# Moving sixteen modulation products from the query stage into the gate stage, and finishing the latent tiles first in the output projection

## The chip, the cores and the metric

The kernel runs on one core of one Trainium2 chip. The metric is the device time of one execution in microseconds; the profile shows one such execution, instruction by instruction, with the time that each engine sat idle and what ended the idling.

## What is computed

Two layers (`DEPTH = 2`) over 256 latent tokens and 256 context tokens of width 1024. Cut to what matters:

```python
for l in range(DEPTH):
    m_lat = split(silu(c) @ ada_w[l] + ada_b[l], 6)        # six modulation rows of 1024
    m_ctx = split(silu(c_ctx) @ ada_w[l] + ada_b[l], 6)
    h  = rmsnorm(x, norm_mix[l]) * (1 + m_lat[1]) + m_lat[0]          # and the same for ctx
    f, p, q, k, v, gates = split_proj(h @ w_in[l])                    # three branches, three gates of 1024
    x  = x + m_lat[2] * ((g0 * yf + g1 * yp + g2 * ya) @ w_out[l])    # ctx too, in layer 0
    h2 = rmsnorm(x, norm_ffn[l]) * (1 + m_lat[4]) + m_lat[3]
    x  = x + m_lat[5] * peer(h2, peer_wq[l], peer_keys[l], peer_u[l], peer_v[l])
```

`peer` makes 8 queries of 256 for each token, scores them against 128 + 128 keys, takes the top 16 of the sums, and mixes the chosen experts of 16,384.

The modulation vector has 6 x 1024 columns. The kernel makes it in three groups of 2048 columns (group 0: `m[0]`, `m[1]`; group 1: `m[2]`, `m[3]`; group 2: `m[4]`, `m[5]`), each as eight products of 128 rows of `ada_w`. One product, `(l, g, k)` below, needs a 1 MB slab of `ada_w`. There are 48 in all.

## The kernel before

All fp32 products on TensorE are made from split operands: `split_to` writes a rounded part `hi` (ScalarE) and the rest `lo` (VectorE, or GpSimd where `pool` is set), and `mm3` (lines 282 to 284) runs three matmuls: hi by hi, one of the mixed products, and the other.

**Weights.** Every weight comes through the class `Stream`. Its list `items` fixes the order of all loads; each item is loaded into one of three buffers of 8 KB a partition (`raw`), issued by SyncE. `take(key)` hands out the next item and issues loads up to two items beyond it; a load waits until the buffer of the item three places earlier has been read. An item that is marked for it is split into a `hl` buffer; `split(key)` hands out a split item and at once splits the next one if that one is marked (`presplit`). Modulation slabs are not split: TensorE reads them from `raw`.

**A modulation product** is `ada_item`: four matmuls of 512 columns, in four column strips of the array, which the profile lists as eight records of line 333 (tile `adaps`). With `k == 0` it also loads the bias (four small loads, line 329). After `k == 7`, `finish` adds the bias on VectorE (line 340, tile `adab`) and SyncE writes the result to DRAM in four pieces (line 346, tile `md`), or `mix_cols` turns it (group 0). After `(0, 2, 7)`, `ffn_rows(0)` follows: SyncE reads rows of `md` back (line 398). Ahead of `(1, 0, 0)` stands `mix_gain(1)`: a small load of `norm_mix` (line 383) and a TensorE transpose of it (line 385).

**Stages of layer 0**, in the order in which they run on TensorE:

- group 0 of layer 0's modulation, the token projections, attention;
- the gate stage: 12 units of `rest`, each 48 matmuls of 512 columns. Ahead of unit `n` stand the modulation products of `ada_at[n]`, two for each unit: the 16 of layer 0's groups 1 and 2, and the 8 of layer 1's group 0;
- the output projection `wout(n, b)`: column block `n` of 4, token tile `b` of 4 (tiles 0 and 1 are latent, 2 and 3 context), then `wout_end(b)`, which stores the tile and computes its norm (`Norm.row`). `Norm.trans(s, q)` and `Norm.cols(s, q)` transpose, modulate and split the normed tiles of side `s` (0 latent, 1 context);
- the query stage: for each head `h` of 8, the query product of `wq` (48 matmuls of 512 columns; in head 0 they are run in two halves, with `nrm.cols(1, ...)` between them), the scores of the head before (tile `SC`), and a share of the top-16 selection on VectorE, handed out by `pump`. In this stage stand the 16 modulation products of layer 1's groups 1 and 2, ahead of the heads: 3, 2, 2, 3, 2, 2, 2;
- the expert stage: 64 steps of `u`, each with a transpose on VectorE (`u_T`, line 1009), splits on ScalarE and GpSimd (`u_hi`, `u_lo`), 48 matmuls and a share of the selection, then 64 steps of `v`.

Instructions of one engine run in the order in which the program writes them (`manual_schedule`). Those lines that the rest turns on:

```python
ada_at[n * len(rest) // 24].append(((0, 1 + n // 8) if n < 16 else (1, 0)) + (n % 8,))   # 242
...
raw_p = sp("raw", 3)
...
self.ahead(self.n + 3)                 # in Stream.take
...
for la, g, k in ada_at[n]:             # gate stage, ahead of each unit
    if (la, g, k) == (1, 0, 0):
        mix_gain(1)
    ada_now(la, g, k)
```

Of the kernel before, what the change touches and what calls it, by code (L numbers as in the profile page):

```python
# [60 lines left out]
def kernel(ctx_: ExitStack, tc: tile.TileContext, I, C, out):  # L61
    nc = tc.nc
    ctx = ctx_
    DEPTH = I["ada_w"].shape[0]
# [45 lines left out]
    def dram(ap_src, off, dims):  # L110
        return bass.AP(tensor=ap_src.tensor, offset=ap_src.offset + off, ap=dims)
# [62 lines left out]
    S = Stream()  # L174
# [5 lines left out]
    def unit_loader(name, l, rows, cols, c0, w=256):  # L180

        def fn(t):
            a = I[name]
            load(out=t[:, :rows // 128 * w].rearrange("p (k n) -> p k n", n=w),
                 in_=dram(a, l * rows * cols + c0, [[cols, 128], [128 * cols, rows // 128], [1, w]]))
        return fn
# [9 lines left out]
    def ada_loader(l, g, k):  # L196
        def fn(t):
            load(out=t, in_=dram(I["ada_w"], (l * D + k * 128) * 6 * D + g * 2048, [[6 * D, 128], [1, 2048]]))
        return fn
# [29 lines left out]
    def const_loader(name, w):  # L229
        def fn(t):  # L230
            load(out=t[:, :w], in_=C[name])
        return fn
# [6 lines left out]
    fills = [("gate", 0, 0), ("gate", 0, 1), ("gate", 0, 2), ("gate", 1, 0)]  # L239
    rest = [("proj", 0, 0)] + [u for u in units[4:] if u not in fills]  # L240
    ada_at = {n: [] for n in range(len(rest))}
    for n in range(24):
        ada_at[n * len(rest) // 24].append(((0, 1 + n // 8) if n < 16 else (1, 0)) + (n % 8,))

    def add_unit(l, u):
        kind, cp, i = u
# [5 lines left out]
    for l in range(DEPTH):  # L252
        if l == 0:
            for k in range(KD):
                S.add(("ada", 0, 0, k), ada_loader(0, 0, k), False)
        for u in (4, 2, 3, 0, 1):
            S.add(("tok", l, u), unit_loader("w_in", l, D, IN_COLS, u * 256), True)
        S.add(("mixc", l), const_loader("mixc", 1280), False)
        S.add(("band", l), const_loader("band", 2048), False)
        for u in fills:  # L260
            add_unit(l, u)
        for n, u in enumerate(rest):
            add_unit(l, u)
            if l == 0:
                for la, g, k in ada_at[n]:
                    S.add(("ada", la, g, k), ada_loader(la, g, k), False)
        for n in range(4):
            S.add(("wout", l, n), unit_loader("w_out", l, D, D, n * 256), True)
        S.add(("keys", l), keys_loader(l), False)
        for h in range(8):  # L270
            S.add(("wq", l, h), wq_loader(l, h), True)
            if l + 1 < DEPTH:
                for n in [n for n in range(16) if n * 7 // 16 == h]:
                    S.add(("ada", l + 1, 1 + n // 8, n % 8), ada_loader(l + 1, 1 + n // 8, n % 8), False)
        for st in range(NSTEP):
            S.add(("u", l, st), u_loader(l, st), False)
        for st in VORDER:
            S.add(("v", l, st), v_loader(l, st), True)
# [73 lines left out]
    def ada_now(l, g, k):  # L352
        f = ada_item(l, g, k)
        if f:
            f()
# [412 lines left out]
    def peer(l, nrm, kT, nb, fin):  # L768
# [261 lines left out]
        for h in range(9):  # L1030
            cur = None
            if h < 8:
                if l + 1 < DEPTH:
                    for n in [n for n in range(16) if n * 7 // 16 == h]:
                        ada_now(l + 1, 1 + n // 8, n % 8)
                wh, wl = S.split(("wq", l, h))
                wh = wh.rearrange("p (k n) -> p k n", n=256)
                wl = wl.rearrange("p (k n) -> p k n", n=256)
                q = b4([128, 2, na], name="q")
                pss = [psum(), psum()]  # L1040
                for c in ([slice(0, 256), slice(256, 512)] if h == 0 and nb == 4 else [slice(0, na)]):
                    if c.start:
                        for q4 in range(4):
                            nrm.cols(1, q4)
                    for p in range(2):
                        w = slice(p * 128, (p + 1) * 128)
                        for k in range(KD):
                            mm3(pss[p][:, c], wh[:, k, w], wl[:, k, w], h2h[:, k, c], h2l[:, k, c], k == 0, k == KD - 1)
                for p in range(2):
                    nc.scalar.activation(q[:, p, :], pss[p][:, :na], AF.Copy)  # L1050
                cur = q
            if prevq is not None:
                g = h - 1
                if g % 4 == 0:
                    SCT[g // 4] = b16([128, 4, 2, nb, 128], name="SC")
                sct = SCT[g // 4][:, g % 4]
                for p in range(2):
                    ps = psum()
                    for b in range(nb):
                        nc.tensor.matmul(ps[:, b * 128:(b + 1) * 128], lhsT=prevq[:, p, b * 128:(b + 1) * 128],  # L1060
                                         rhs=kT[:, 2 * g + p, :], start=True, stop=True)
                    nc.scalar.activation(sct[:, p], ps[:, :na].rearrange("p (b n) -> p b n", b=nb), AF.Copy)
                SC[g] = sct
                if g == 3 and sparse is not None:
                    token_rows()
                if g == 5:
                    u_T(0)
                if g == 6:
                    u_hi(0)
                    u_lo(0)  # L1070
                if g == 7:
                    for q in range(1, LEAD):
                        u_T(q)
                        u_hi(q)
                        u_lo(q)
                    u_T(LEAD)
                pump((15.0 if g < 5 else 9.0) if nb == 4 else (5.6 if g < 6 else 3.0))
            prevq = cur
# [111 lines left out]
    nrm = Norm(0, X, 4, False)  # L1190
# [11 lines left out]
    for l in range(DEPTH):  # L1202
        last = l == DEPTH - 1
        nb = 2 if last else 4
# [3 lines left out]
        def keys():  # L1208
            kT = b8([128, 16, 128], name="keysT")
            for q in range(4):  # L1210
                ps = psum()
                for a in range(4):
                    nc.tensor.transpose(ps[:, a * 128:(a + 1) * 128], kr[:, 4 * q + a, :], ident)
                nc.scalar.activation(kT[:, 4 * q:4 * q + 4, :], ps.rearrange("p (a n) -> p a n", a=4), AF.Copy)
            return kT
# [9 lines left out]
        nrm = Norm(l, X, nb, True)  # L1225
        xm = [dr_p.tile([128, D], F32, name=f"xm{l}_{b}") for b in range(nb)]

        def wout(n, b):
            wh = wo[n][0].rearrange("p (k n) -> p k n", n=256)
            wl = wo[n][1].rearrange("p (k n) -> p k n", n=256)  # L1230
            c = slice(n * 256, (n + 1) * 256)
            ps = psum()
            t = slice(b * 128, (b + 1) * 128)
            for k in range(KD):
                m = mg[k // 4][:, :, k % 4, t]
                mm3(ps[:, :256], m[:, 0], m[:, 1], wh[:, k, :], wl[:, k, :], k == 0, k == KD - 1)
            tm = b1([128, 256], name="tm")
            nc.vector.tensor_tensor(out=tm, in0=ps[:, :256], in1=m2[b // 2][:, c], op=OP.mult)
            nc.vector.tensor_tensor(out=X[:, b, c], in0=X[:, b, c], in1=tm, op=OP.add)

        def wout_end(b):
            nc.sync.dma_start(out=xm[b], in_=X[:, b, :])
            nrm.row(b // 2, b % 2)
# [5 lines left out]
                wout(n, b)  # L1249
        if nb == 4:  # L1250
            wo[2] = S.split(("wout", l, 2))
            for b in range(nb):
                wout(2, b)
            wo[3] = S.split(("wout", l, 3))
            kr = S.take(("keys", l)).rearrange("p (a d) -> p a d", d=128)
            for b in range(2):
                wout(3, b)
            wout_end(0)
            wout(3, 2)
            wout_end(1)  # L1260
            S.presplit(True)
            wout(3, 3)
            kT = keys()
            for q in range(4):
                nrm.trans(0, q)
            for b in (2, 3):
                wout_end(b)
            for q in range(4):
                nrm.cols(0, q)
        else:  # L1270
            wo[2] = S.split(("wout", l, 2))
            wo[3] = S.split(("wout", l, 3))
            kr = S.take(("keys", l)).rearrange("p (a d) -> p a d", d=128)
            wout(2, 0)
            wout(3, 0)
            wout_end(0)
            S.presplit(True)
            wout(2, 1)
            wout(3, 1)
            wout_end(1)  # L1280
            kT = keys()
            for q in range(4):
                nrm.cols(0, q)
# [35 lines left out]
        if not last:  # L1319
            nrm = nxt["nrm"]  # L1320
# [29 lines left out]
```

## Time and profile before

| | |
|---|---|
| three runs | 3004.71, 3005.0, 3011.52 us; median 3005.0 |
| the profiled execution | 3004.79 us; its span in the trace 3002.7 us |
| mean granted TensorE clock | 0.958 of full speed |
| busy over the span | TensorE 92%, VectorE 70%, ScalarE 46%, GpSimd 43% |
| traffic | 235 GB/s mean over the span |

Times in the trace count from the start of the span. A busy share says only how much of a stretch an engine worked; what sets the time is read from the waits: an engine's row in brackets shows how long it sat idle just before the instruction, and which engine or transfer ended that. L12 is line 12 of the program. DMA-issuing instructions on SyncE's queue are marked SPq.

### The profile page before, as it was taken

The page shows a single profiled execution, that of the slowest core. Times are in us where ns is not written, and L with a number is a line of the kernel's source. Part 1 is how long each engine was busy: PE and PEld are TensorE (multiplying, and loading weights), DVE is VectorE, ACT ScalarE, POOL GpSimd, SP SyncE. Part 2 cuts the span into 40 slices and gives each one's busy share as a digit, 9 for nine tenths or more (in the row PEclk, how much of TensorE's full clock was granted, in tenths as well). Part 3 has the DMA queues.
Part 4 walks back from the last instruction along what each step waited for, and adds up shares of the span by engine and source line. Part 5 has one row for each costly group of instructions (what it writes and reads, how often), then busy time and mean ns, then how long its engine had stood idle before and what let it go on. Part 6 is the DMA issues. An engine that isn't in the chain of part 4 may idle for free. (4 is left out here: it accounts for less than half of the span.)

```text
span 3002.7 us, 42583 instructions
## 1 busy us (share of the span) xinstructions
PE 2753.9 (92%) x16484; PEld 2419.2 (81%) x16484; DVE 2114.1 (70%) x3252; ACT 1372.8 (46%) x2243; POOL 1287.1 (43%) x674
## 2 busy tenths in 40 slices
PE   6999998798887879999999998899887998899999
PEld 4767786688887779988888887779887988888887
DVE  3444355898787765558999997646797889466666
ACT  3443222233488874333333333444444777544443
POOL 0110002247666557766666664110577676610000
PEclk8999999899988989999999999999998999999999
DMA  6215655657987879999999996426788799987775
GB/s 228 89 39 201 243 175 167 173 135 192 238 240 231 256 242 290 283 291 392 368 384 373 365 385 249 143 84 198 148 182 187 197 237 229 224 288 294 285 291 202
DMA packets 365579, 706.98 MB, mean 235 GB/s; under 512 B 25425, under 2 KB 265457, under 8 KB 351297
## 3 DMA queue, kind: packets, MB, share of 16 engines
q1 hardware_dynamic: 271104, 491.38, 54.8%
q0 software_dynamic: 36864, 134.23, 12.5%
q10 hardware_dynamic: 57408, 78.65, 7.6%
q8 instruction: 129, 2.11, 0.3%
q14 instruction: 74, 0.60, 0.1%
HBM read 619.18 MB, written 85.00 MB: 235 GB/s over the span
## 5 line engine op out<-in xcount | busy, mean ns | idle before, releaser
L1173 PE MATMUL acc<-hl,A 128*128 128x512 f32 x3840 | 870.9, 389 | 0.0
L1173 PEld LDWEIGHTS acc<-hl,A 128*128 128x128 f32 x3840 | 720.6, 188 | 149.9 <-ACT A L287 0.2
L1023 POOL TENSOR_TENSOR hl<-UT,hl 128x1024 fp32r<-128x1024 f32 x256 | 656.9, 2591 | 357.1 <-ACT hl L1016 348.6
L289 POOL TENSOR_TENSOR hl<-raw,hl 128x1024 fp32r<-128x1024 f32 x112 | 277.9, 2491 | 694.0 <-ACT hl L287 573.2
L287 ACT ACTIVATE hl<-raw 128x1024 fp32r<-128x1024 f32 x388 | 387.8, 1048 | 220.1 <-PE acc L1173 84.5
L289 DVE TENSOR_TENSOR hl<-raw,hl 128x1024 fp32r<-128x1024 f32 x276 | 354.1, 1315 | 120.8 <-ACT hl L287 120.4
L282 PE MATMUL ps<-hTh,hl 128*128 128x384 f32 (+2 forms) x1168 | 416.2, 356 | 24.7 <-ACT stg L924 17.9
L284 PE MATMUL ps<-hTh,hl 128*128 128x384 f32 (+2 forms) x1168 | 410.7, 352 | 9.1 <-POOL hl L1023 8.7
L283 PE MATMUL ps<-hTl,hl 128*128 128x384 f32 (+2 forms) x1168 | 409.7, 351 | 3.5 <-POOL hTl L289 3.5
L1009 DVE STREAM_TRANSPOSE UT<-raw 128x2048 f32<-128x2048 f32 x128 | 294.4, 2301 | 142.4 <-DMA raw<-in_peer_u_dram 110.0
L1016 ACT ACTIVATE hl<-UT 128x1024 fp32r<-128x1024 f32 x256 | 256.3, 1049 | 223.8 <-DVE UT L1009 207.6
L282 PE MATMUL ps<-hT,hl 128*128 128x256 f32 x1152 | 336.9, 292 | 20.5 <-ACT Hg L1128 13.2
L284 PE MATMUL ps<-hT,hl 128*128 128x256 f32 x1152 | 334.6, 290 | 16.7 <-POOL hl L1023 16.7
L283 PE MATMUL ps<-hT,hl 128*128 128x256 f32 x1152 | 333.0, 289 | 1.1 <-POOL hT L289 1.1
L282 PEld LDWEIGHTS ps<-hTh,hl 128*128 128x128 f32 x1168 | 231.8, 198 | 40.6 <-ACT stg L924 21.3
L287 ACT ACTIVATE A<-af 128x768 fp32r<-128x768 f32 (+1 forms) x128 | 94.5, 738 | 344.3 <-PE acc L1173 182.8
L282 PEld LDWEIGHTS ps<-hT,hl 128*128 128x128 f32 x1152 | 228.7, 199 | 23.3 <-ACT Hg L1128 15.0
L284 PEld LDWEIGHTS ps<-hTh,hl 128*128 128x128 f32 x1168 | 230.7, 197 | 18.3 <-POOL hl L1023 13.5
L284 PEld LDWEIGHTS ps<-hT,hl 128*128 128x128 f32 x1152 | 228.3, 198 | 20.1 <-POOL hl L1023 20.1
L962 DVE SCALAR_TENSOR_TENSOR picked<-picked,hrow 128x1024 f32<-128x1024 f32 x128 | 152.8, 1209 | 126.1 <-DMA picked<-in_peer_u_dram,picks 125.7
L283 PEld LDWEIGHTS ps<-hTl,hl 128*128 128x128 f32 x1168 | 231.9, 199 | 8.0 <-POOL hTl L289 3.7
L283 PEld LDWEIGHTS ps<-hT,hl 128*128 128x128 f32 x1152 | 228.5, 198 | 1.6 <-POOL hT L289 1.6
(246 smaller groups left out, 4651.8 us busy)
## 6 DMA issues: line engine op xcount, KB each, us to landing
raw<-in_peer_u_dram SPq DMA_DIRECT2D x512, 256.0 KB
raw<-in_peer_v_dram SPq DMA_DIRECT2D x128, 1024.0 KB
raw<-in_ada_w_dram SPq DMA_DIRECT2D x48, 1024.0 KB
G<-stg ACTq DMA_DIRECT2D x20, 2048.0 KB
raw<-in_w_in_dram SPq DMA_DIRECT2D x34, 1024.0 KB
Gq<-G SPq DMA_DIRECT2D x16, 1536.0 KB
H<-Hg ACTq DMA_DIRECT2D x56, 384.0 KB
Hq<-H SPq DMA_DIRECT2D x14, 1536.0 KB
```

Of the source, the lines that this page charges most:

```text
L282: nc.tensor.matmul(ps, lhsT=lh, rhs=rh, start=first, stop=False)
L283: nc.tensor.matmul(ps, lhsT=lh, rhs=rl, start=False, stop=False)
L284: nc.tensor.matmul(ps, lhsT=ll, rhs=rh, start=False, stop=last)
L287: nc.scalar.activation(hi, src, AF.Copy)
L289: eng.tensor_tensor(out=lo, in0=src, in1=hi.bitcast(F32), op=OP.subtract)
L962: nc.vector.scalar_tensor_tensor(row, row, 1.0, SP["h"], op0=OP.mult, op1=OP.mult, accum_out=dots[:, k:k + 1])
L1009: nc.vector.transpose(t, r)
L1016: nc.scalar.activation(t[:, 0, a], v[:, a], AF.Copy)
L1023: nc.gpsimd.tensor_tensor(out=t[:, 1, a], in0=v[:, a], in1=t[:, 0, a].bitcast(F32), op=OP.subtract)
L1173: nc.tensor.matmul(acc[b][n], lhsT=a4[:, lhs, a, t], rhs=rhs[:, o:o + 512], start=f, stop=e)
```

## The change

It does two things. The 16 modulation products of layer 1's groups 1 and 2 leave the query stage and join the 24 that stand in layer 0's gate stage: 40 over 12 units, which comes to 4, 3, 3, 4, 3, 3, 4, 3, 3, 4, 3, 3. The list of loads changes alike. And in layer 0's output projection, column blocks 2 and 3 are no longer run one after the other over all four tiles: both latent tiles are taken through blocks 2 and 3 first and normed, the transposes of the keys and of the latent side and its `cols` are put among the last products of the context tiles.

```diff
-    for n in range(24):
-        ada_at[n * len(rest) // 24].append(((0, 1 + n // 8) if n < 16 else (1, 0)) + (n % 8,))
+    for n in range(40):
+        ada_at[n * len(rest) // 40].append(((0, 1 + n // 8) if n < 16 else (1, n // 8 - 2)) + (n % 8,))
@@ list of loads, query stage
-            if l + 1 < DEPTH:
-                for n in [n for n in range(16) if n * 7 // 16 == h]:
-                    S.add(("ada", l + 1, 1 + n // 8, n % 8), ada_loader(l + 1, 1 + n // 8, n % 8), False)
@@ query stage, ahead of head h
-                if l + 1 < DEPTH:
-                    for n in [n for n in range(16) if n * 7 // 16 == h]:
-                        ada_now(l + 1, 1 + n // 8, n % 8)
@@ output projection, four tiles
             wo[2] = S.split(("wout", l, 2))
-            for b in range(nb):
-                wout(2, b)
             wo[3] = S.split(("wout", l, 3))
             kr = S.take(("keys", l)).rearrange("p (a d) -> p a d", d=128)
             for b in range(2):
+                wout(2, b)
                 wout(3, b)
-            wout_end(0)
+                wout_end(b)
+            S.presplit(True)
+            wout(2, 2)
             wout(3, 2)
-            wout_end(1)
-            S.presplit(True)
-            wout(3, 3)
             kT = keys()
+            wout(2, 3)
             for q in range(4):
                 nrm.trans(0, q)
+            for q in range(4):
+                nrm.cols(0, q)
+            wout(3, 3)
             for b in (2, 3):
                 wout_end(b)
-            for q in range(4):
-                nrm.cols(0, q)
```

## Rows read from the trace of the kernel before

**Rows 1.** Busy us of each engine (instructions) in the gate stage; then granted clock, DMA, GB/s.

```profile
238.40:395.90 157.50, 156.63 (x775) 112.83 (x774) 59.58 (x80) 43.12 (x54) 0.52 (x1) 1.00 0.71 250
```

**Rows 2.** Timeline of VectorE, from the first selection to the expert stage: start, us, instruction, [idle before].

```profile
494.35 0.29 DVE L791 MAX8 T1v<-SC 128x8 f32<-128x128 f32 x1 [19.94 <-ACT SC L1062]
...
540.61 0.29 DVE L791 MAX8 T1v<-SC 128x8 f32<-128x128 f32 x1 [7.69 <-ACT SC L1062]
...
580.33 0.29 DVE L791 MAX8 T1v<-SC 128x8 f32<-128x128 f32 x1 [1.79 <-ACT SC L1062]
581.17 0.68 DVE L791 MAX8 T1v<-SC 128x8 f32<-128x128 f32 x3 [0.54 <-ACT SC L1062]
...
591.14 0.66 DVE L340 TENSOR_TENSOR adab<-adaps,adab 128x512 f32<-128x512 f32 x1
...
629.07 2.28 DVE L1009 STREAM_TRANSPOSE UT<-raw 128x2048 f32<-128x2048 f32 x1
```

**Rows 3.** Timeline of ScalarE and TensorE at the third expert step.

```profile
631.38 2.00 ACT L1016 ACTIVATE hl<-UT 128x1024 fp32r<-128x1024 f32 x2 [9.02 <-DVE UT L1009]
...
632.49 0.63 PE L282 MATMUL ps<-hTh,hl 128*128 128x384 f32 x1 [2.33 <-ACT hl L1016]
```

**Rows 4.** Waits of SyncE's queue in the query stage: us in total, times, longest.

```profile
SPq L346 <- DVE adab L340: 35.6, 2, 27.2
```

**Rows 5.** Timeline of TensorE in the query stage: a modulation product after its load.

```profile
539.52 1.94 PE L333 MATMUL adaps<-raw,cT 128*32 128x512 f32 x8 [14.58 <-DMA raw<-in_ada_w_dram]
```

**Rows 6.** Timeline of TensorE: two modulation products in a row, and three.

```profile
329.39 1.92 PE L333 MATMUL adaps<-raw,cT 128*32 128x512 f32 x16
...
509.27 2.78 PE L333 MATMUL adaps<-raw,cT 128*32 128x512 f32 x24
```

**Rows 7.** A gate-stage load: SyncE's issues, and the stretch (last column GB/s).

```profile
304.52 1.19 SPq L198 DMA_DIRECT2D raw<-in_ada_w_dram  x2
...
304.50:308.60 4.10, 4.10 (x23) 2.74 (x16) 2.36 (x2) 1.80 (x2) 0.00 (x0) 1.00 0.76 256
```

**Rows 8.** Timeline of SyncE and TensorE at the kernel's start, the first eight products.

```profile
2.39 0.29 SPq L383 DMA_DIRECT2D mrows<-in_norm_mix_dram  x1
...
3.93 0.27 PE L385 MATMUL ps<-ident,mrows 8*128 8x8 f32 x1
...
9.70 11.86 SPq L198 DMA_DIRECT2D raw<-in_ada_w_dram  x5
...
16.74 1.94 PE L333 MATMUL adaps<-raw,cT 128*32 128x512 f32 x8 [3.03 <-DMA raw<-in_ada_w_dram]
```

**Rows 9.** Timeline of SyncE's queue around product (0, 2, 7).

```profile
330.52 0.33 SPq L198 DMA_DIRECT2D raw<-in_ada_w_dram  x1
332.16 1.15 SPq L346 DMA_DIRECT2D md<-adab  x4
...
337.12 0.32 SPq L383 DMA_DIRECT2D mrows<-in_norm_mix_dram  x1
```

**Rows 10.** TensorE after a short wait, and the stretch behind it (third column from the end: granted clock).

```profile
612.00 0.62 PE L284 MATMUL ps<-hTh,hl 128*128 128x384 f32 x1 [1.81 <-POOL hl L1023]
...
612.00:616.00 4.00, 4.00 (x14) 4.00 (x15) 4.00 (x15) 1.72 (x2) 2.87 (x2) 0.57 0.12 35
```

**Rows 11.** Timeline of TensorE between the output projection and head 0's second half.

```profile
454.72 4.64 PE L333 MATMUL adaps<-raw,cT 128*32 128x512 f32 x24 [8.30 <-DVE hTf L472]
...
468.12 0.66 PE L451 MATMUL ps<-ident,xn 128*128 128x128 f32 x4 [1.51 <-ACT hTf L474]
...
472.68 0.58 PE L283 MATMUL ps<-hTl,hl 128*128 128x256 f32 x1 [3.51 <-POOL hTl L289]
```

**Rows 12.** Timeline of GpSimd and VectorE: splits that TensorE waits for.

```profile
466.29 4.66 POOL L289 TENSOR_TENSOR hl<-raw,hl 128x1024 fp32r<-128x1024 f32 x2 [10.08 <-ACT hl L287]
...
385.50 2.36 DVE L289 TENSOR_TENSOR hl<-raw,hl 128x1024 fp32r<-128x1024 f32 x2
...
398.61 0.69 DVE L289 TENSOR_TENSOR mg<-gt,mg 128x512 fp32r<-128x512 f32 x1 [0.70 <-ACT mg L287]
```

## The prediction

> **What bounds the kernel now.** I read the busy times by stretch first. In the gate stage TensorE works 156.6 of 157.5 us [rows 1]: what is added there lengthens the stage, unless it waits besides. Then I read the waits. In the query stage TensorE once stands still for 14.58 us for a slab of `ada_w` [rows 5]. The slab is late because SyncE's queue, which issues every load in order, stands at the write of `md`, and that waits for VectorE's bias sum `adab`, 27.2 us at the longest [rows 4]: the sum is queued behind the top-16 selection. So the place from which the products are taken really has a fault.
>
> What that fault is worth is a second question. From the first selection at 494.35 VectorE is busy almost without a break: it idles when scores are late (7.69, 1.79 and 0.54 us [rows 2]) and otherwise works through to the transposes of the experts' first slabs. At the third expert step TensorE waits 2.33 us for ScalarE, and ScalarE has waited 9.02 us for VectorE's transpose of 629.07 [rows 2, 3]. So the query stage ends, for what comes after, when VectorE is through with its list, not when TensorE is. A gain on TensorE there counts only as far as VectorE starts earlier or idles less.
>
> **Added to the gate stage: 16 products.** Two in a row take 1.92 us, three 2.78 [rows 6]: 0.86 us for each further one. 16 x 0.86 = **+13.8 us**, with nothing to hide it, TensorE being full there.
>
> **Added waits: the fourth product of a unit.** Three `raw` buffers let two items be under way beside the one in use. With two products to a unit the ring holds exactly both slabs and the next unit's weights. With three it holds the three slabs when their turn comes; the unit's weights, and two slabs of the next turn, are then fetched during the 11 us of the unit, and the last slab when the weights have been split. I take this as just fitting: the last slab's load begins some 10 us into a period of about 14 and needs about 5 (below); the first two slabs of the turn cover the rest. With four slabs it can't fit: the fourth may be loaded only when the first is used up. SyncE issues that load 1.13 us after the turn begins (330.52 against 329.39 [rows 6, 9]). A slab needs 4.1 us from issue to the last byte on an idle queue (256 GB/s x 4.1 us = 1.05 MB [rows 7]); I add 1.0 us until TensorE sees it, an estimate from the kernel's start, where an issue at 9.70 serves a product at 16.74, 7.0 us later with two slabs ahead of it [rows 8]. So it is there 6.2 us after the turn began, and TensorE is through with three slabs after 2.78: a wait of 3.4 us. Bounds: 2.4 without the extra microsecond, 5.4 with the 7.0 us of the start. Behind the waiting product stands the whole unit; nothing else can run on TensorE.
>
> A short wait costs more than itself. After one of 1.81 us the granted clock falls to its lower level, 1.2 GHz: in the four us behind it, it averages 0.57 [rows 10], so 1.7 us of full-speed work are lost. I count 1.7 behind each wait, 0 as the bound. Units 0, 3, 6 and 9 have four products: 4 x (3.4 + 1.7) = **+20.4 us** (9.6 to 28.4).
>
> The Trainium skill, DMA: Bandwidth & Descriptors, section Anatomy of one DMA, fits a transfer as 2.0 us plus its bytes over 436 GB/s, which makes 4.4 us for a slab. By it the four waits would be 2.7 us each and the sum 2.8 us lower; the row gives 4.1 before any completion, and my sum keeps 5.1.
>
> **Moved past SyncE's queue: `mix_gain(1)`.** Product (0, 2, 7) and product (1, 0, 0) stood in different units, with 48 matmuls between them. Now both are in unit 4's turn: numbers 14, 15 and 16. After number 15 SyncE waits for the bias sum, writes `md`, waits until that has landed, reads the rows back, and only then issues the `norm_mix` rows, whose transpose stands ahead of number 16 on TensorE. In the rows that load is issued at 337.12, 5.8 us after number 15 ended (329.39 + 1.92), 0.4 of it a slab load that will stand elsewhere [rows 6, 9]. The same load took 1.5 us from issue to its transpose at the kernel's start [rows 8]. TensorE waits 5.4 + 1.5 = 6.9 us, with the clock 8.6: **+8.6 us** (6.4 to 11). Slabs are late there too, but inside this wait.
>
> **The stage's end.** The weights of output block 0 are now loaded into the buffer of the last unit's first slab. Issued 1.1 us into the turn, landed at 6.2 (their shorter rows make it rather 6.7), they are split by VectorE up to about 10 us into it, 4 us before TensorE leaves the stage at 13.9. Before, that split began at 385.50 and ended 8 us ahead of 395.9 [rows 1, 12]. Behind it on VectorE stand the last unit's six gate products, four sums and two splits, some 0.69 us each with 0.70 us of ScalarE ahead of each split [rows 12]: 9.7 us. The last split of `mg`, which the first output product needs about 3 us in, came 3.4 us in before and comes 5.7 in now. A wait of 2.5, with the clock **+4.2 us** (0 to 5).
>
> **Removed between output projection and head 1.** Before, TensorE stands idle 8.30 us for the latent norm, then runs three products in 4.64 [rows 11]. Now the latent tiles' norm falls behind four output products and the keys, and the transposes stand ahead of the last product. I take the whole wait as hidden. In head 0 the context side remains: its tiles now end last, its norm chain ends about 1 us after the first half of the head, and its low parts stand on GpSimd behind the split of head 1's weights, 4.66 us [rows 12]. That leaves some 4.1 us of the 1.51 + 3.51 [rows 11]. With the two products ahead of head 1 (1.85, counting their overlap): 8.3 + 4.6 + 0.9 + 1.85 = **-15.6 us** for the first scores, counted from the end of the gate stage. Bounds: -19.7 if the context wait goes too, -8 if half the latent wait is back.
>
> **Removed on VectorE.** With the products gone no `md` write stands in SyncE's queue, so scores come in time: 13.1 us for a head on TensorE against some 18 of selection. The idle 7.69 + 1.79 + 0.54 and two sums of 0.66 fall out [rows 2]: 11.3 us. TensorE's own removed time, 14.58 us and ten products more, is cover here and gives nothing beyond: TensorE merely waits longer at the third step. **-11.3 us** (-12 to -5, if another wait takes a part). Later stages have the same order of work and shift as a whole. The bias sums and `md` writes in the gate stage cost nothing more: VectorE is busy 59.6 of 157.5 us there [rows 1].
>
> **Sum.** 13.8 + 20.4 + 8.6 + 4.2 - 15.6 - 11.3 = +20.1 us. The profiled execution took 3004.8 (span 3002.7, 2.1 around it), 0.2 from the median of 3005.0: **3025 us**.
>
> **Rivals.**
> *The ring keeps up.* All waits in the gate stage vanish: 13.8 - 15.6 - 11.3 = -13.1, 2992 us. It needs a slab within 1.65 us of its issue (2.78 - 1.13), against 4.1 for the bytes alone, and the `norm_mix` rows ahead of time. With waits of W us in all the change gives W - 13.1; it is faster by over 0.3% (9 us, about what a measurement of this kernel can tell from no change) only where W stays under 4.1 us; I forecast 33.2. For it speaks only that three slabs never made TensorE wait in the query stage's second such turn [rows 6]. Chance 0.07.
> *Short waits, no clock.* W = 4 x 2.4 + 6.4 = 16, nothing at the stage's end: +2.9, 3008 us. Against it: 1.81 us of waiting sufficed for the clock [rows 10]. Chance 0.15.
> *VectorE's gain doesn't arrive*, because the step after is bound by something that the trace shows only as hidden now: +11.3 on the forecast, 3036 us. Against it: the chain of rows 2 and 3. Chance 0.10.
>
> The forecast has 0.68, with its own range 3013 to 3036. The bounds together give 3003 to 3046. The range 3002 to 3043 leaves out the fastest rival and the far end of the third. Faster by over 0.3%: 0.07; within it 0.17, the second rival and a bit of the forecast's low end; slower 0.76.
>
> **What would show it.** In the changed trace: the gate stage some 47 us longer, with four waits of `adaps` for a slab of 2.4 to 5.4 us in units 0, 3, 6 and 9, one of about 7 us before the `mix_gain` transpose in unit 4, and the granted clock at its lower level behind each; 8.3 us of idle gone ahead of head 0; no idle on VectorE from the first scores to the third expert step, and a longer wait of TensorE there. The prediction is wrong if `raw` slabs arrive in the turn, if TensorE reaches unit 4's transpose after its rows, or if the third step doesn't follow VectorE.

## The result and the profile after

The change makes the kernel slower: 3031.5 us (median of 5 runs, 3030.3 to 3043.7) against 3004.7 (5 runs, 3000.8 to 3011.5), a ratio of 1.0091 with a 95% interval of 1.0074 to 1.0108, or +26.8 us. The profiled execution took 3030.3 us, its span is 3028.5. Behind the edits its line numbers are 3 to 6 lower than before.

I cut both traces at the same events: the first modulation product of the gate stage, the first matmul of the output projection, the first `MAX8` of the selection, VectorE's transpose for the third expert step (629.07 in [rows 2]), the first of the 64 `v` steps, the end. The steps of `u` and of `v` are those of the expert stage. The gate stage before (before, e2, e10, e11) and the stretch from the first selection to the third expert step (the changed kernel, e1, e3 to e6) repeat to 0.1 us between kernels that share their code. The changed gate stage, with its waits, doesn't: it takes 202.7 to 206.9 us in the four kernels that have it as it is (the changed kernel, e1, e7, e12).

| us | before | after | difference | forecast |
|---|---|---|---|---|
| gate stage | 157.54 | 205.38 | +47.8 | +42.8 |
| its end to the first selection | 98.38 | 84.11 | -14.3 | +4.2 - 15.6 = -11.4 |
| first selection to third expert step | 134.72 | 134.29 | -0.4 | -11.3 |
| rest of the `u` steps | 712.0 | 705.4 | -6.6 | 0 |
| `v` steps and layer 1 | 1661.6 | 1660.6 | -1.0 | 0 |

**Gate stage.** First the busy times by stretch: us of TensorE, its weight loads, VectorE, ScalarE, GpSimd (instructions), then granted clock, DMA share, GB/s. The first line answers to [rows 1]; the next four are stretches in and behind the waits of units 3, 4, 6 and 9.

```profile
238.69:444.07 205.38, 181.87 (x904) 121.77 (x903) 59.60 (x79) 44.19 (x54) 1.05 (x2) 0.93 0.75 267
290.00:298.00 8.00, 5.27 (x23) 2.45 (x16) 0.71 (x1) 1.80 (x2) 0.00 (x0) 0.57 0.98 332
310.00:322.00 12.00, 5.12 (x17) 2.85 (x18) 3.73 (x5) 2.32 (x3) 0.24 (x1) 0.57 0.66 207
352.00:360.00 8.00, 7.13 (x24) 5.54 (x21) 3.58 (x9) 2.11 (x2) 0.52 (x1) 0.57 1.01 394
400.00:408.00 8.00, 6.87 (x22) 4.20 (x23) 2.16 (x2) 2.00 (x2) 0.00 (x0) 0.57 1.02 380
```

TensorE was full before (156.63 of 157.50). Now it stands idle for 23.5 us of a longer stage, and in the four stretches the granted clock is 0.57 on average. The waits themselves are in TensorE's timeline (start, us, instruction, idle before it and what ended that):

```profile
238.69 2.78 PE L330 MATMUL adaps<-raw,cT 128*32 128x512 f32 x24
244.78 1.06 PE L330 MATMUL adaps<-raw,cT 128*32 128x512 f32 x8 [3.31 <-DMA raw<-in_ada_w_dram]
...
289.59 1.07 PE L330 MATMUL adaps<-raw,cT 128*32 128x512 f32 x8 [2.76 <-DMA raw<-in_ada_w_dram]
293.39 1.94 PE L330 MATMUL adaps<-raw,cT 128*32 128x512 f32 x8 [2.73 <-DMA raw<-in_ada_w_dram]
...
296.27 0.63 PE L281 MATMUL ps<-yh,hl 128*128 128x512 f32 x1
...
297.92 0.39 PE L279 MATMUL ps<-yh,hl 128*128 128x512 f32 x1
...
316.88 0.24 PE L382 MATMUL ps<-ident,mrows 8*128 8x8 f32 x1 [7.42 <-DMA mrows<-in_norm_mix_dram]
...
351.25 1.06 PE L330 MATMUL adaps<-raw,cT 128*32 128x512 f32 x8 [3.08 <-DMA raw<-in_ada_w_dram]
...
401.13 1.94 PE L330 MATMUL adaps<-raw,cT 128*32 128x512 f32 x8 [3.14 <-DMA raw<-in_ada_w_dram]
...
448.09 0.38 PE L279 MATMUL ps<-hl,mg 128*128 128x256 f32 x1 [1.25 <-ACT mg L284]
```

(A turn is the row of products ahead of a unit.) Each turn of four products waits for its last slab, unit 3's for the last two. The same matmul takes 0.63 us behind a wait and 0.39 when the clock is back. On SyncE's queue stand the issues that end three of these waits:

```profile
239.82 0.35 SPq L198 DMA_DIRECT2D raw<-in_ada_w_dram  x1
...
312.86 2.17 SPq L395 DMA_DIRECT2D mrows<-md  x4
...
315.41 0.30 SPq L380 DMA_DIRECT2D mrows<-in_norm_mix_dram  x1
...
396.33 0.33 SPq L198 DMA_DIRECT2D raw<-in_ada_w_dram  x1
```

The fourth slab is issued 1.13 us into the turn and used 4.96 us (unit 0) and 4.80 us (unit 9) after its issue; the `norm_mix` rows 1.47 us after theirs. Unit 3 is the exception: its third slab was used 7.05 us after its issue, and its fourth 7.71. In unit 2's turn an `md` write and a bias load stand on SyncE's queue, and the first two slabs of unit 3 were issued 6.0 and 6.4 us after that turn began, where unit 2's own had been issued 2.0 and 2.9 after the one before. That this is why they were late is read from the order of the issues; no run tested it.

**From the first selection on.** The same stretch by engine, columns as above, of the kernel before and after:

```profile
494.35:629.07 134.72, 117.35 (x646) 94.85 (x645) 123.91 (x636) 31.34 (x44) 34.09 (x15) 0.92 0.55 145
```

```profile
528.18:662.47 134.29, 108.73 (x563) 95.56 (x561) 133.69 (x635) 31.53 (x44) 33.57 (x14) 0.90 0.28 59
```

VectorE's idle time did go, from 10.8 to 0.6 us, but its busy time rose by 9.8 us, with the two bias sums gone from it. The groups of VectorE's instructions by line (busy us, mean ns of one, idle before) show which took it, before and after:

```profile
L812 DVE TENSOR_TENSOR cand<-T1v 128x256 f32<-128x256 f32 x24 | 13.8, 611 | 0.0
```

```profile
L809 DVE TENSOR_TENSOR cand<-T1v 128x256 f32<-128x256 f32 x24 | 25.2, 1088 | 0.0
```

The `cand` adds of the selection make pairwise sums of two top-16 lists; they took 11.4 us more. One pair of them on VectorE's timeline before, with nothing beside it on GpSimd:

```profile
574.13 0.40 DVE L812 TENSOR_TENSOR cand<-T1v 128x256 f32<-128x256 f32 x1
...
574.45 0.41 DVE L812 TENSOR_TENSOR cand<-T1v 128x256 f32<-128x256 f32 x1
```

And one after:

```profile
543.73 1.70 DVE L809 TENSOR_TENSOR cand<-T1v 128x256 f32<-128x256 f32 x1
...
545.36 2.62 DVE L809 TENSOR_TENSOR cand<-T1v 128x256 f32<-128x256 f32 x1
```

GpSimd's timeline at that time, the low parts of the next head's query weights:

```profile
542.75 2.40 POOL L286 TENSOR_TENSOR hl<-raw,hl 128x1024 fp32r<-128x1024 f32 x1 [7.92 <-ACT hl L284]
...
545.10 2.59 POOL L286 TENSOR_TENSOR hl<-raw,hl 128x1024 fp32r<-128x1024 f32 x1
```

GpSimd's two end at 545.15 and 547.69, the two adds 0.28 and 0.29 later. An add that should take 0.4 us lasts until the GpSimd instruction beside it is over, and the profile books all of it as busy. The Trainium skill, SBUF — State Buffer, section "SBUF: two separate sides", states a rule that fits this: VectorE and GpSimd share one pair of SBUF ports under an exclusive lock; of a VectorE operation with two SBUF inputs and a GpSimd instruction that reads SBUF, the one that starts first keeps the pair for its whole length, and the other waits. The traces agree, here at 2.62 us for 0.41. The other order stands in the trace of before: a pair of adds that began at 565.12, 0.15 us ahead of GpSimd's split, took its usual 0.73 us, and the split 2.83 instead of 2.4.

TensorE, meanwhile, waits for VectorE. Its timeline at the first expert step and at the third, which answers to [rows 3]:

```profile
627.47 0.69 PE L279 MATMUL ps<-hTh,hl 128*128 128x384 f32 x1 [14.02 <-ACT hl L1013]
...
665.90 0.45 PE L279 MATMUL ps<-hTh,hl 128*128 128x384 f32 x1 [4.06 <-ACT hl L1013]
```

### The profile page after: what moved, and what is told of

Same layout as the page of the kernel before. It is cut to its first block, busy times and chain, and to the rows that moved or that the text cites. A ratio compares the mean times of both kernels' runs of the same rounds, so it can differ in the third digit from the quotient of the medians.

```text
span 3028.5 us, 42571 instructions
## 1 busy us (share of the span) xinstructions
PE 2760.8 (91%) x16484; PEld 2424.9 (80%) x16484; DVE 2129.0 (70%) x3252; ACT 1374.8 (45%) x2243; POOL 1288.3 (43%) x674
## 5 line engine op out<-in xcount | busy, mean ns | idle before, releaser
L279 PE MATMUL ps<-hTh,hl 128*128 128x384 f32 (+2 forms) x1168 | 415.5, 356 | 47.3 <-ACT hl L1013 27.2
L279 PE MATMUL ps<-hT,hl 128*128 128x256 f32 x1152 | 337.6, 293 | 17.9 <-ACT Hg L1122 11.3
L281 PE MATMUL ps<-hT,hl 128*128 128x256 f32 x1152 | 335.3, 291 | 16.7 <-POOL hl L1020 16.7
L959 DVE SCALAR_TENSOR_TENSOR picked<-picked,hrow 128x1024 f32<-128x1024 f32 x128 | 152.6, 1208 | 121.4 <-DMA picked<-in_peer_u_dram,picks 121.4
```

Of the source, the lines that this page charges most:

```text
L279: nc.tensor.matmul(ps, lhsT=lh, rhs=rh, start=first, stop=False)
L281: nc.tensor.matmul(ps, lhsT=ll, rhs=rh, start=False, stop=last)
L959: nc.vector.scalar_tensor_tensor(row, row, 1.0, SP["h"], op0=OP.mult, op1=OP.mult, accum_out=dots[:, k:k + 1])
```

## The experiments

Four groups: the two parts alone, the waits of the gate stage, VectorE's adds, and combinations. The table gives for each profiled execution the stage times in the cuts above, the busy time of the 24 `cand` adds, and the measured ratio.

| kernel | gate stage | to first selection | to third expert step | `cand` adds | third expert step at | median us, runs | ratio, 95% interval |
|---|---|---|---|---|---|---|---|
| before | 157.5 | 98.4 | 134.7 | 13.8 | 629.1 | 3004.7, 5 | |
| after | 205.4 | 84.1 | 134.3 | 25.2 | 662.5 | 3031.5, 5 | 1.0091 (1.0074 to 1.0108) |
| e1 | 205.5 | 92.9 | 134.3 | 25.2 | 671.2 | 3051.4, 4 | 1.0144 (1.0125 to 1.0164) |
| e2 | 157.5 | 94.1 | 135.1 | 16.7 | 626.2 | 2995.2, 5 | 0.9966 (0.9949 to 0.9982) |
| e3 | 197.9 | 83.8 | 134.3 | 25.2 | 654.0 | 3026.6, 4 | 1.0060 (1.0042 to 1.0079) |
| e4 | 191.1 | 82.7 | 134.3 | 25.2 | 646.9 | 3021.2, 10 | 1.0050 (1.0033 to 1.0066) |
| e5 | 186.3 | 82.3 | 134.3 | 25.2 | 640.4 | 3006.8, 1 | |
| e6 | 187.2 | 83.2 | 134.3 | 25.2 | 644.3 | 3013.1, 10 | 1.0028 (1.0017 to 1.0039) |
| e7 | 202.7 | 83.7 | 124.0 | 14.8 | 650.5 | 3022.4, 5 | 1.0056 (1.0037 to 1.0076) |
| e8 | 183.9 | 82.9 | 123.9 | 14.8 | 630.0 | 3002.2, 12 | 0.9995 (0.9983 to 1.0008) |
| e9 | 178.5 | 84.1 | 121.4 | 12.2 | 623.0 | 2997.2, 9 | 0.9969 (0.9957 to 0.9981) |
| e10 | 157.6 | 93.0 | 132.2 | 23.1 | 622.4 | 2994.2, 10 | 0.9974 (0.9962 to 0.9985) |
| e11 | 157.6 | 98.3 | 123.4 | 14.3 | 619.3 | 2989.0, 6 | 0.9953 (0.9941 to 0.9965) |
| e12 | 206.9 | 83.3 | 134.6 | 14.2 | 664.3 | 3036.6, 1 | |

The runs of the kernel before that stood beside e1 to e4 have a median of 3005.9, those beside e5 to e8 3004.9, those beside e9 to e12 3003.5; the ratios are taken to these. The rest of the `u` steps takes 702 to 716 us, and the `v` steps with layer 1 1658 to 1667, whatever the kernel, so a total holds 14 us and more that no stage of the change decides; the stage times are the finer instrument, save that a gain of under some 4 us on the changed gate stage can't be told from its own spread (above).

### e1: the products alone

The products stand in the gate stage, the output projection keeps its old order.

> Only the sixteen products are moved; the output projection runs in the old order. Theory (ring waits in the gate stage, and VectorE's gain in the query stage eaten by adds that wait for GpSimd): the gate stage is about 48 us longer than before, the 8.3 us idle ahead of head 0 is back, and from the first scores to the third expert step it takes as long as in the changed kernel, about 134 us; some 8 to 10 us above the changed kernel, 3038 to 3042 us. Rival (the new order of the output projection is what takes VectorE's gain): that stretch falls to about 124 us, and the time is at or under the changed kernel, 3026 to 3031 us.

The gate stage and the stretch behind the first selection are those of the changed kernel. The new order is worth 92.9 - 84.1 = 8.8 us of its -14.3; the products that left this stretch give the rest. The idle ahead of head 0 is back, 8.19 us. The total misses the expectation of 3038 to 3042: the third expert step comes 8.7 us later than in the changed kernel, but all four times lie 16 to 23 us above that kernel's median. In the profiled execution the rest of the `u` steps took 715.0 us, 9.5 more; why, no run shows.

### e2: the order alone

The output projection's new order, the products where they were.

> Only the output projection runs in the new order; the products stay where they were. Theory: about 9 us less from the end of the gate stage to the first scores (the 8.3 us idle goes), the wait of 14 us for a slab stays; 2995 to 2999 us. Rival (a start of the selection at another moment changes its waits for GpSimd as much as the change did): the gain is lost again between the first scores and the third expert step, 3003 to 3008 us.

Faster by 0.34%, in the range expected. But only 4.3 us are gained ahead of the first selection, where about 9 were expected and e1's comparison gives 8.8. Here the slabs of the query stage still pass SyncE, and the new order puts the two latent tiles' stores early on that queue. SyncE's queue in this kernel:

```profile
442.26 8.06 SPq L1242 DMA_DIRECT2D xm<-X  x2
450.37 0.43 SPq L198 DMA_DIRECT2D raw<-in_ada_w_dram  x1
```

And TensorE's timeline:

```profile
456.67 1.93 PE L333 MATMUL adaps<-raw,cT 128*32 128x512 f32 x8 [5.12 <-DMA raw<-in_ada_w_dram]
```

The slab's load stands 8 us behind stores that wait for VectorE, and TensorE then waits 5.12 us for it. Of the 10.7 us between the medians, 2.9 are there by the third expert step; the others fall into the later stages, which vary by more than that.

### e3: the `norm_mix` rows loaded early

```diff
+                if n == 1:
+                    mix_rows(1)        # the load of mrows; the transpose stays in mix_gain(1)
```

> The changed kernel, with the small load of the norm_mix rows issued in unit 1 and its transpose left where it is. Theory: the 7.4 us wait of unit 4 and the slow clock behind it go, about 9.8 us, with no new wait above 1 us: 3020 to 3023 us. Rival (the slabs of unit 5, late by the same queue, then make TensorE wait): only 3 to 6 us gained, 3025 to 3028 us, with a wait of 2 to 4 us for a slab in unit 5.

The 7.42 us wait is gone. The stage is 7.45 us shorter than the changed kernel's, 4.8 to 8.9 by that stage's spread, and the time, 3026.6, lies in the rival's range. TensorE's timeline in units 3 and 5:

```profile
287.38 1.07 PE L330 MATMUL adaps<-raw,cT 128*32 128x512 f32 x8 [0.85 <-DMA raw<-in_ada_w_dram]
...
290.38 1.06 PE L330 MATMUL adaps<-raw,cT 128*32 128x512 f32 x8 [1.94 <-DMA raw<-in_ada_w_dram]
...
294.08 1.94 PE L330 MATMUL adaps<-raw,cT 128*32 128x512 f32 x8 [2.64 <-DMA raw<-in_ada_w_dram]
...
324.60 1.06 PE L330 MATMUL adaps<-raw,cT 128*32 128x512 f32 x8 [0.78 <-DMA raw<-in_ada_w_dram]
...
327.11 1.07 PE L330 MATMUL adaps<-raw,cT 128*32 128x512 f32 x8 [1.44 <-DMA raw<-in_ada_w_dram]
```

Unit 3 comes before the wait that the edit removes, and its waits are those of the changed kernel in other portions (5.4 us in all, 5.5 there). Unit 5's are new, 0.78 and 1.44 us, as the rival had it: the long wait seems to have let the loads catch up too.

### e4: the fourth product inside the unit

```diff
-                for la, g, k in ada_at[n]:
+                for t in ada_at[n][:3]:        # three ahead of the unit, as before
...
+                    inner(at, (5,))            # the fourth after 5 of a gate unit's 8 column groups
...
+                    inner(3 * c + i, (4,))     # or after group 4 of a projection unit
```

The fourth slab also moves behind the next unit's weights in the list of loads.

> The changed kernel, with the fourth product of units 0, 3, 6 and 9 placed about three quarters into the unit instead of ahead of it, and its slab behind the next unit's weights in the list of loads. Theory (the wait is the ring's: the fourth load can start only when the first slab is used up): the waits of 3.3, 5.5, 3.1 and 3.1 us and their slow clock go, 18 to 23 us: 3009 to 3014 us. Rival (the loads as a whole are too much for the stage): the waits come back elsewhere in the gate stage, which shortens by under 8 us: 3024 us or more.

The stage is 14.3 us shorter, less than the theory's 18 to 23, and the time, 3021.2, lies between those of theory and rival. In the units' turns the waits of 2.7 to 3.3 us are gone; the `norm_mix` wait stays (7.48 us), and smaller waits for slabs stand in its place, 1.80, 0.95 and 1.74 us.

### e5: both

> The fourth product inside the unit and the norm_mix rows loaded early, together. Theory: the two gains add, since the waits stand in different units: gate stage 205.4 - 7.5 - 14.3, that is 183 to 185 us; from there to the third expert step as in the changed kernel. Rival (one ring: what one removal frees, the next wait takes): 188 us or more.

e3 and e4 together: 186.3 us, 19.1 below the changed kernel and, within the spread, the theory's 183 to 185. Seven waits for slabs are left, 0.61 to 2.19 us, 10.2 in all: where nothing long holds TensorE up any more, three buffers don't carry three products to a turn without waits.

### e6: one product ahead of a unit, the others at its quarters

Early rows as in e3; `inner` at groups 1, 3, 5 of a gate unit (1, 2, 4 of a projection unit).

> All products spread over their unit: one ahead of it, the others after each further quarter; norm_mix rows loaded early. Theory (only the burst is at fault, the stage's loads fit): the gate stage comes near 157.5 + 13.8 = 171.3 us plus a little, 172 to 177 us, with the clock at full speed; the time falls by 25 to 30 us against the changed kernel, to the level of the kernel before or just under it (the expert stage wanders by some 14 us from one execution to the next). Rival (52 MB of loads are too much for the stage): 183 us or more, with waits for slabs all over it.

The stage time that I expected, 172 to 177, is missed, and the total falls by 18 us, not 25 to 30, though the waits are nearly gone. TensorE's timeline around the only one for a slab:

```profile
315.41 1.07 PE L333 MATMUL adaps<-raw,cT 128*32 128x512 f32 x8
316.41 0.50 PE L282 MATMUL gate<-hTh,hl 128*128 128x512 f32 x1
...
323.19 1.06 PE L333 MATMUL adaps<-raw,cT 128*32 128x512 f32 x8 [3.76 <-DMA raw<-in_ada_w_dram]
```

The slab that it waits for was issued at 315.97, behind a read of `md` at which SyncE stood for 5.37 us. The rest is the price of a product by itself. Counted from start to start it takes 1.00 us where 0.86 was reckoned, and the 12 matmuls of a quarter of a unit behind it 2.95 us, where a unit in one piece takes 11.12 / 4 = 2.78. That makes some 0.3 us for each of 28 more places than in the changed kernel, 8 us, and the one wait with the clock behind it 5: 13 of the 15.9 us above 171.3.

### e7: GpSimd's splits in pieces of 256 columns

The changed kernel with `lo` of the query weights made in four GpSimd instructions in place of one, so that no add waits for longer than a piece.

```diff
+        for o in range(0, 1024, fine):          # fine = 256 in layer 0's query stage
+            w = slice(o, o + fine)
+            eng.tensor_tensor(out=lo[:, w], in0=src[:, w], in1=hi[:, w].bitcast(F32), op=OP.subtract)
```

> The changed kernel, with GpSimd's split of the query weights cut into pieces of 256 columns instead of 1024; nothing else. Theory (VectorE's adds of the selection, tile cand, wait for the GpSimd instruction that runs beside them to end): the 24 pairs that took 25.2 us take 12 to 16 us, and the stretch from the first scores to the third expert step falls from 134.3 to 123 to 127 us. Rival (the adds are slow for another reason, or the stretch is bound by TensorE): cand stays over 22 us, the stretch over 132 us.

As the theory said (the group has 24 adds, 12 pairs; the expectations of e7 and e12 call the adds pairs). VectorE's group in this kernel, and the stretch by engine:

```profile
L815 DVE TENSOR_TENSOR cand<-T1v 128x256 f32<-128x256 f32 x24 | 14.8, 657 | 0.0
```

```profile
526.53:650.49 123.96, 107.44 (x563) 94.43 (x561) 123.36 (x635) 31.57 (x44) 38.85 (x44) 0.93 0.30 64
```

The adds are back at 14.8 us and the stretch is 10.3 us shorter than the changed kernel's, 10.8 shorter than before. This is the -11.3 of the prediction. GpSimd pays for it, 38.85 us against 33.57, where nobody waits.

### e12: the query weights split on VectorE

The changed kernel with `S.pool = nb != 4`, which takes GpSimd out of the collision.

> The changed kernel with the split of the query weights made by VectorE in place of GpSimd. Theory (the adds wait for a GpSimd instruction): with no GpSimd work in the heads the 24 pairs of adds take 9 to 13 us instead of 25.2; VectorE gets 6 to 7 splits of 2.4 us more, so that the stretch is 131 to 136 us. Rival (the adds are slow because of their operands' place in memory or of the transfers): they still take over 20 us, and the stretch grows to 147 us or more.

```profile
L809 DVE TENSOR_TENSOR cand<-T1v 128x256 f32<-128x256 f32 x24 | 14.2, 636 | 0.0
...
L286 DVE TENSOR_TENSOR hl<-raw,hl 128x1024 fp32r<-128x1024 f32 x10 | 11.7, 1214 | 0.0
```

With the query splits off GpSimd the adds fall to 14.2 us, a little above the 9 to 13 expected (two pairs still collide with GpSimd's splits of expert slabs), and VectorE's own splits cost 11.7: the stretch stays at 134.6. So in the changed kernel VectorE loses about as much time by waiting for GpSimd as it would take to do the work itself.

### e10 and e11: the bias sum off VectorE, products where they were

Instead of moving the products, the sum that held up SyncE is moved: e2, with layer 1's bias sums of groups 1 and 2 made by a ScalarE copy from PSUM and a GpSimd add. e11 has e7's fine splits besides.

```diff
+            if l and g:
+                nc.scalar.activation(bt[:, 1, :], ps, AF.Copy)
+                nc.gpsimd.tensor_tensor(out=bt[:, 1, :], in0=bt[:, 1, :], in1=bt[:, 0, :], op=OP.add)
```

> The new order of the output projection alone, the products in the query stage as before, but the bias sums of layer 1's groups 1 and 2 made by ScalarE and GpSimd instead of VectorE. Theory (the query stage's fault was only that SyncE's queue stood behind VectorE's selection): no wait for a slab above 6 us in the query stage, no idle above 1 us on VectorE from the first scores on, and that stretch at 123 to 134 us against 135.1, according to how its adds fall beside GpSimd's splits; the gate stage stays 157.5 us; 2985 to 2997 us. Rival (the loads of products and query weights together are late anyway): waits for slabs of 5 us or more remain in several heads, and the stretch is at 135 us or above.

> The same with GpSimd's splits of the query weights in pieces of 256 columns. Theory: the adds take 12 to 16 us in all, the stretch from first scores to third expert step 123 to 126 us; the third step comes 10 us or more before that of the new order alone; 2980 to 2990 us, faster than both kernels. Rival: the stretch stays above 130 us.

VectorE's adds in e10 and in e11:

```profile
L816 DVE TENSOR_TENSOR cand<-T1v 128x256 f32<-128x256 f32 x24 | 23.1, 1005 | 0.0
```

```profile
L822 DVE TENSOR_TENSOR cand<-T1v 128x256 f32<-128x256 f32 x24 | 14.3, 637 | 0.0
```

In e10 VectorE's idle time falls to 0.6 us as in the changed kernel, and the adds again take 23.1 us, with all products still in the query stage: the collisions don't need the products to be moved. What both kernels share is VectorE's run without a break beside GpSimd. e11 is the fastest kernel of the study, 0.9953 of before, with 14.3 us for the adds and the gate stage untouched. Its third expert step comes 6.9 us before e2's, though, not the 10 or more that were expected: its way to the first selection is 5.3 us longer than e10's: GpSimd needs 6.0 us for eight pieces, not 4.7 for two wholes, so the low parts of the context tiles come later (TensorE waits 3.10 us for them, 1.32 in e10), and the wait for a slab is 6.47 us, not 3.21.

### e8 and e9: the change with its faults mended

e8 is e6 with the fine splits. e9 runs products in pairs, two ahead of a unit and two in its middle in 8 of 12 units, with early rows and fine splits.

> The spread products, the early rows and the fine splits together. Theory: both gains stand, gate stage 172 to 177 us, 123 to 127 us from first scores to third expert step, so that the third step is reached 5 to 12 us before that of the kernel before, and the time is 2990 to 3000 us. Rival (VectorE's stretch is bound otherwise once the gate stage is shorter): no better than the spread products alone.

> As the run with spread products, early rows and fine splits, but the products in pairs: two ahead of a unit and, in eight of the twelve units, two more at its middle. Theory (a product between two gate matmul groups costs its own 1.0 us and the change over, about 1.2 us; in a pair 1.0; the loads fit): the gate stage takes 174 to 180 us against 183.9, with no wait above 1.5 us, and the third expert step comes 4 to 10 us earlier. Rival (what is left above 171 us is waiting for loads, not the change over): 184 us or more.

e8 is no faster than before: 3002 misses the expected time, because the gate stage still costs 26 us more (183.9, where 172 to 177 were expected) and the other two stretches give 26 back. e9's gate stage, 178.5 us, lies where the theory put it, with no wait for a slab above 1.16 us; 157.5 + 13.8 = 171.3 would be the floor. It beats the kernel before by 0.31%, but not e11, which gets nearly the same gain on VectorE without paying 21 us in the gate stage.

## Why the prediction came out as it did

**Direction and time.** 3025 was forecast, 3031.5 measured. By the terms, for the profiled execution: 20.1 forecast, +5.0 in the gate stage, -2.9 at its end, +0.1 behind it, +10.9 on VectorE, -7.6 in the later stages, and the stage begins 0.3 later: 25.9 in all, against 25.8 between the two spans. That the total is only 6.5 us off is in part luck: +10.9 and -7.6, the two largest deviations, have opposite signs, and nothing in the sum foresaw either. The terms' upper bounds add up to 3050, not 3046 as the prediction has it.

**The products** cost what was counted, 0.86 us each in a row; six that run alone behind a wait take 1.06 at full clock, together 1.2 us more.

**The ring of three buffers** worked as described, and the waits measured 3.31, 2.76 + 2.73, 3.08 and 3.14: 15.0 us against 4 x 3.4 = 13.6. The slab is used 6.1 us (unit 0) after the turn began, forecast 6.2, and 4.96 after its issue, where the sum kept 5.1; the 4.1 in it was misread, though: [rows 7] have two issues, so two slabs shared the 1.05 MB of that stretch, and that 4.1 + 1.0 fits is partly luck. The Trainium skill (DMA: Bandwidth & Descriptors, Anatomy of one DMA) gives 2.0 us plus the bytes over 436 GB/s as a fit for transfers from GpSimd's queue; taken as an estimate for SyncE's loads here, its 4.4 us is a little short of the 4.80 to 4.96 measured. What was wrong is that three slabs just fit: in unit 3 the third was late as well, used 7.05 us after its issue where 5 was reckoned. e4 and e5 show what else the ring lacks.

**The clock** was sized too low where it fell, and once it didn't fall. By starts of a unit's first matmul and of the next product, units 3, 4, 6 and 9 run 12.28, 12.42, 13.58 and 13.00 us for 11.10 in unit 0: 6.9 us, and 3.0 more in the products and transposes that stand right behind the waits. That is 9.9 in four places, 2.5 each; 1.7 was forecast for each of five. Together with the terms above and below, 13.8 + 1.2 + 15.0 + 7.4 + 9.9 = 47.3, measured 47.8; the rest is short delays inside the rows of products of units 3, 6 and 10.

**`mix_gain(1)`** moved past SyncE's queue as forecast: 7.4 us of waiting for 6.9. e3, which moves nothing but this load, removed it, and 7.45 us of the stage (4.8 to 8.9 by its spread).

**The stage's end** was sized too high: 1.25 us, with no fall of the clock, for 2.5 + 1.7. The weights were split by 9.9 us into the turn, as forecast, but the list behind them took VectorE 9.0 us for 9.7, and TensorE left the stage at 14.25 for 13.9: the last split of `mg` ended 4.7 us into the output projection, not 5.7.

**Between output projection and first scores** 14.3 us were gained, or 15.5 without the 1.25: the forecast was 15.6. The 8.30 us ahead of head 0 [rows 11] are gone but for 2.25, where none were forecast; on the context side the waits are 0.46, 0.96 and 0.42 us, where 4.1 were forecast. The two errors cancel, so the agreement of this term is luck too. TensorE's timeline there:

```profile
498.11 0.35 PE L279 MATMUL ps<-hTh,hl 128*128 128x256 f32 x1 [2.25 <-DVE tm L1232]
...
509.13 0.39 PE L280 MATMUL ps<-hTl,hl 128*128 128x256 f32 x1 [0.96 <-POOL hTl L286]
```

**VectorE: the step that failed.** The prediction said that the idle 7.69 + 1.79 + 0.54 us and two sums fall out, 11.3 us. They did fall out, and the third expert step still came only 0.4 us sooner. The sum took the durations of VectorE's instructions as given; they depend on what GpSimd does beside them. e7 shows the cause: the same kernel with shorter GpSimd instructions gains the 10.3 us. e10 shows that it comes without the moved products too, and e12 that GpSimd's query splits are the main partner (of the seven held pairs below, five met one, two a split of expert slabs). Before, 4 of the 12 pairs of adds were held by a GpSimd split, after 7, and three of those were held by two splits in a row, for 4.2 to 4.4 us a pair instead of 0.74. Heads on TensorE now come about every 13 us and bring a split each, and in the first heads VectorE comes to a pair of adds every 12.5 us or so; a pair that isn't held comes 9.0 us after the one before it, so some 3.5 of the 12.5 us are the wait itself, which keeps the next pair in step with the next head's splits. That this rhythm makes them meet so often is my reading of the timeline, which no run varied by itself.

The third rival, that VectorE's gain doesn't arrive, had its place and its time, 3036, nearer to the truth at this step than the forecast; its reason, a bound in the stage behind, was not the one. The first two rivals are out: the waits are there, and so is the clock. The remaining -7.6 us of later stages lie within the 14 us by which the rest of the `u` steps varies, and I give them no cause. One regularity stays open: in all kernels with the new order that were timed more than once the median is better, by 0.3 to 8 us, than the shift of the third expert step would make it; in e1, which has the old order, it is 3 us worse.

## What to carry to other kernels

Idle time on a neighbour engine is not a gain until its instructions have been priced for the overlap that they will then have: here VectorE's two-input adds waited out the GpSimd splits that had begun before them, the wait counted as busy, and cutting the GpSimd work into short pieces removed most of it. Work that moved into a stage with a full TensorE cost its own time, and with a ring of three buffers also a wait for each transfer beyond what the ring holds; the small load queued behind a write and its read-back deserved an early issue. When one late sum holds a queue, try to move the sum before you move the work behind it: e10 does so, at 0.9974, and e11 with fine splits, at 0.9953.

## What the runs showed of the hardware

- A VectorE add of 0.4 us took up to 2.62 us beside a GpSimd `TENSOR_TENSOR` of 2.6 that had begun before it, and ended 0.28 to 0.29 us after it.
- TensorE's granted clock stayed at its upper level behind a wait of 3.31 us (unit 0; in e3, behind 3.36 us at the same place, it fell), and fell to 1.2 GHz in or behind waits of 3.08 and 3.14 us (units 6 and 9), of 3.76 (e6) and, in [rows 10], of 1.81; in unit 3 it stayed behind the first of two waits, 2.76, and fell in the second, 2.73. The length of a single wait did not tell whether it falls.
- A modulation product between two groups of full-width matmuls took 1.00 us from start to start, and the 12 matmuls behind it 2.95 (e6), against 0.86 for one more product in a row and 2.78 for a quarter of an unbroken unit.
- Four GpSimd pieces of 256 columns took 2.8 us where one instruction of 1024 took 2.4, and 3.2 to 3.5 beside the adds (e7, e11), where the one took up to 2.8.
